# A one-core mixer block with split fp32 weights: order of the leading and trailing products, fewer LayerNorm visits, a shorter last normalisation

## The chip, the cores and the metric

One core of a Trainium2 chip runs the whole program. The metric is device time in microseconds (us) of one execution, less is better. Engines are called PE (TensorE matmul), PEld (its weight load), DVE (VectorE), ACT (ScalarE), POOL (GpSimd) and SP (SyncE), as the profile does.

## What is computed

One layer with 256 latent and 256 context tokens of 2048 channels. After RMSNorm and adaLN, one input projection feeds a convolution branch (GLU, depthwise convolution of width 31, LayerNorm over channels, swish, a SiLU gate) and a bidirectional gated recurrence; both go through a projection, are merged by sigmoid gates, and an output projection, a gated residual and a last RMSNorm follow:

```python
v = v + p["conv_dw_b"]
v = jax.nn.silu(layernorm(v, p["conv_ln_g"], p["conv_ln_b"]))
y_conv = (v * jax.nn.silu(z)) @ p["w_conv_out"]
y_rnn = ((hf + hb) * jax.nn.silu(z_r)) @ p["w_rnn_out"]
y = jax.nn.sigmoid(gc) * y_conv + jax.nn.sigmoid(gr) * y_rnn
x = x + gt[:, None] * (y @ p["w_o"])
return rmsnorm(x, final_g)
```

## The kernel before

Every fp32 weight and activation is split into a leading part (fp32r, "hi") and a remainder ("lo"), and a product is the sum of three: hi by hi, hi by lo, lo by hi. Weights come in slots `s` of 1 MB, each of two halves `h` (128 x 1024, 512 KB). `stage_load(s + 3)` has SP fetch the raw halves of a slot three ahead; `stage_split(s + 2, h)` splits a half two slots ahead: ACT copies it into `whi` (L184), and DVE subtracts that from the raw half into `wlo` (L189). To spare DVE, one half in four of the slots 24 to 103 (`adding`, L383) gets its `wlo` another way: ACT writes the negated, rounded weight into `wlo` (L195), and POOL then issues a DMA that adds the raw weight from HBM onto it (L196). There are four buffers of each kind, so the split of half (s + 2, h) starts when PE has read the half (s, h) for the last time.

The first 72 slots multiply weights as the stationary operand. The last 80 are five chunked stages of 16 slots, in the order gr, rnn, gc, conv, o: there the activations `xx` (`xh`, `xl`) are stationary, the weights stream with 512 columns, and the two token tiles `i` (128 tokens each) have one PSUM accumulator each. `chunk_mms` (L607) makes the six matmuls of one half for one token tile, and `chunk_slot` (L616) calls it for tile 0 and then tile 1:

```python
for w, y in ((hi, xh), (hi, xl), (lo, xh)):
    for kk in range(2): ...
```

so that a half is hi x4, lo x2 (tile 0), hi x4, lo x2 (tile 1). A chunk of 512 output columns takes four slots; then `evac` empties the two accumulators (DVE and ACT). The o stage does the same in its own loop (L1045 to L1067), and does its last two slots for tile 0 first, then tile 1.

The order of work on every engine is the order of the program. Between halves, `run_deferred` runs what was put off by a half, and `run_side` takes elementwise work (convolution taps on DVE, LayerNorm steps) from a queue, as much as a budget per slot allows. LayerNorm needs sums over channels, which are on partitions: `stat_mm` (L236) is an fp32 matmul with a 128 x 32 block of ones at column position 32 x (m mod 4), 256 columns wide, and shows as two instructions in the trace. For the means it is called in pairs of channel tiles (`mean`, L719: seven visits at tap 10 of the pairs, one at the end), for the variances once for each of 16 squares (`var`, L793), which run_deferred gathers into visits. After each sum a matmul with `sel4` adds the four quarters (`ln_total`), DVE copies the total to SBUF, and for the variance `rsqrt` (L205: ACT square root, DVE reciprocal and one Newton step) follows. Then the normalised tiles are gated and split; this must be done before the conv stage (L974).

In the o stage, `evac_o` (L1015) adds the residual, takes the square sum by ACT into `ssq`, and multiplies by the final weight; `finish` (L1032) computes the row's reciprocal root with `rsqrt`, scales the four column pieces on DVE and ACT in turn and has SP write them. `turn` (L978) transposes the merged result for the o stage while conv runs.

Of the kernel before, what the change touches and what calls it, by code (L numbers as in the profile page):

```python
# [15 lines left out]
P = 128  # L16
# [68 lines left out]
def block_kernel(ctx, tc, xcat, xtok, fgrow, brow, par, wada, wgt, bgt, wearly, wall, wgate, out):  # L85
# [335 lines left out]
    def defer(n, f):  # L421

        queue[n].append(f)
# [180 lines left out]
            k = 8 * half + kk  # L604
            PE.matmul(out=acc[:, 0], lhsT=lo[:, 128 * kk:128 * kk + 128], rhs=xh[:, k, 1], start=False, stop=(k == KT - 1))  # L605

    def chunk_mms(acc, s, seg, kq, h, i):  # L607

        hi, lo = parts[s, h]
        for w, y in ((hi, xh), (hi, xl), (lo, xh)):  # L610
            for kk in range(2):
                k = 4 * kq + 2 * h + kk
                PE.matmul(out=acc, lhsT=y[:, k, seg, P * i:P * i + P], rhs=w[:, 512 * kk:512 * kk + 512],  # L613
                          start=(k == 0 and w is hi and y is xh), stop=(k == KT - 1 and w is lo))

    def chunk_slot(s, seg, accs, kq, budget):  # L616

        stage_load(s + 3)
        for h in range(2):
            for i in range(2):  # L620
                chunk_mms(accs[i], s, seg, kq, h, i)
            del parts[s, h]
            stage_split(s + 2, h)
            run_deferred()
            run_side(budget / 2)
# [63 lines left out]
    def open_ph2():  # L689
        nonlocal cv, zc, tp2, p2  # L690
        ph1.close()
        cp = ph2.enter_context(tc.tile_pool(name="conv", bufs=1))
        tp2 = ph2.enter_context(tc.tile_pool(name="ctmp", bufs=2))
        cv = cp.tile([P, KT, T], F32, name="cv")
        zc = cp.tile([P, KT, T], F32, name="zc")
        p2 = cp.tile([P, KT, T], F32, name="p2")
        for n in ("rstd", "mean", "var"):
            ln[n] = tp2.tile([P, T], F32, tag=n, name=n, bufs=1)

    cv = zc = tp2 = p2 = mps = None  # L700
# [3 lines left out]
    def conv_ops(ms):  # L704
        ops = []

        def first(m):
            A.activation(out=cv[:, m], in_=vb[:, m], func=AF.Identity,  # L708
                         scale=hdw[:, m * CW + 15:m * CW + 16], bias=pc("dwb", m))

        def tapop(m, j):
            d = j - 15
            n = GW - abs(d)
            o0, i0 = max(0, -d), max(0, d)
            o = cv[:, m].rearrange("p (r c) -> p r c", c=GW)[:, :, o0:o0 + n]
# [3 lines left out]
        def mean(m):  # L719
            nonlocal mps  # L720
            if m == 0:
                mps = psum("mps")[:, :T]
            stat_mm(mps, cv[:, m], m)
# [52 lines left out]
        V.tensor_copy(ln["rstd"], mps)  # L776
        defer(0, ln_mean2)

    def ln_total(dst):
        tot = psum("tot")[:, :T]  # L780
        PE.matmul(out=tot, lhsT=sel4, rhs=ln["rstd"], start=True, stop=True)
        V.tensor_copy(dst, tot)

    def ln_mean2():
        ln_total(ln["mean"])
        side.extend((0.4, lambda m=m: ln_center(m)) for m in range(KT))

    def ln_center(m):
# [4 lines left out]
        def var():  # L793
            nonlocal vps
            if m == 0:
                vps = psum("vps")[:, :T]
            stat_mm(vps, sq, m)
            if m == KT - 1:
                defer(0, ln_var)
        defer(0, var)  # L800
# [203 lines left out]


    ssq = tp2.tile([P, 2, 4], F32, tag="ssq", name="ssq", bufs=1)
    rt = tp2.tile([P, 2], F32, tag="rt", name="rt", bufs=1)
    rn = tp2.tile([P, 2], F32, tag="rn", name="rn", bufs=1)
    ms2 = tp2.tile([P, 2, 2], F32, tag="ms2", name="ms2", bufs=1)
    A.activation(out=rn[:, 0:1], in_=epst, func=AF.Sqrt)  # L1010

    def ochunk(c, i):
        return xo[:, 2048 * i + 512 * c:2048 * i + 512 * c + 512]

    def evac_o(c, i, acc):  # L1015
        while c not in gt_done:
            gt_steps(1)
        o = ochunk(c, i)
        j = 2 * (2 * c + i)
        t = vb[:, j:j + 2].rearrange("p a t -> p (a t)")  # L1020
        V.scalar_tensor_tensor(out=t, in0=acc, scalar=0.5, in1=gtb[:, 512 * c:512 * c + 512], op0=MUL, op1=MUL)
        V.tensor_tensor(out=o, in0=o, in1=t, op=ADD)
        A.activation(out=t, in_=o, func=AF.Square, scale=2048.0 ** -0.5, accum_out=ssq[:, i, c:c + 1])
        V.tensor_tensor(out=o if c < 3 else last(i), in0=o, in1=fgb[:, 512 * c:512 * c + 512], op=MUL)
# [4 lines left out]
    def last(i):  # L1029
        return piece(p2v, 0, i)  # L1030

    def finish(i):  # L1032

        r, v = rn[:, i:i + 1], ms2[:, i, 1:2]
        V.tensor_tensor(out=v, in0=ms2[:, i, 0:1], in1=ssq[:, i, 3:4], op=ADD)
        rsqrt(r, rt[:, i:i + 1], v)
        for c in (3, 0, 1, 2):
            o = ochunk(c, i) if c < 3 else last(i)
            if c % 2:
                V.tensor_scalar(out=o, in0=o, scalar1=r, scalar2=None, op0=MUL)  # L1040
            else:
                A.activation(out=o, in_=o, func=AF.Copy, scale=r)
            SP.dma_start(out=out[i, :, 512 * c:512 * c + 512], in_=o)

    for c in range(4):  # L1045
        accs = [psum(f"o{c}{i}") for i in range(2)]
        for kq in range(2 if c == 3 else 4):
            stage_load(s + 3)
            for h in range(2):
                for i in range(2):  # L1050
                    chunk_mms(accs[i], s, 1, kq, h, i)
                del parts[s, h]
                stage_split(s + 2, h)
                gt_steps(GTO)
                if turns:
                    turn(turns.popleft())
            s += 1
        if c < 3:
            for i in range(2):
                evac_o(c, i, accs[i])  # L1060

    stage_split(NS, 0)
    for i in range(2):
        for q in range(2):
            for h in range(2):
                chunk_mms(accs[i], s + q, 1, 2 + q, h, i)
        evac_o(3, i, accs[i])  # L1067
        finish(i)
    ph2.close()
# [77 lines left out]
```

## Time and profile before

| what | value |
|---|---|
| median of 3 runs (lowest, highest) | 1137.34 us (1136.67, 1138.25) |
| the profiled execution, its own time | 1136.45 us |
| its span, first to last instruction | 1134.7 us |
| busy PE, PEld, DVE, ACT | 1103.8, 879.8, 902.8, 656.4 us |
| granted TensorE clock, mean | 0.993 |
| DMA, mean over the span | 226 GB/s |

The span leaves out 1.75 us of the execution's own time. The ends of matmuls are modelled: a matmul of 512 columns is shown as 0.39 us long though they follow each other faster, so starts are compared here, and a gap printed in brackets is shorter than the delay of the start. Rows of the timeline merge instructions of one kind; "x4" is four of them.

### The profile page before, as it was taken

What the parts mean: (1) busy time and instruction counts of PE and PEld (TensorE: products, weight loads), DVE (VectorE), ACT (ScalarE), POOL (GpSimd) and SP (SyncE); (2) the same over time, 40 slices, a digit from 0 to 9 for tenths busy, and PEclk for the clock granted to TensorE, in tenths of its full rate; (3) what the DMA queues carried; (4) which work ended last, traced back from release to release, by engine and by line L of the source; (5) the groups of instructions that cost most, each with busy time, mean ns of one, the idle gap of its engine ahead of it and who ended that gap; (6) DMA issues with size and microseconds to landing.
All of it is one profiled execution on the core that took longest, in us unless ns stands there. A gap on an engine that the chain in (4) does not pass through costs nothing.

```text
span 1134.7 us, 15866 instructions
## 1 busy us (share of the span) xinstructions
PE 1103.8 (97%) x5788; PEld 879.8 (78%) x5788; DVE 902.8 (80%) x1544; ACT 656.4 (58%) x894; POOL 34.8 (3%) x44
## 2 busy tenths in 40 slices
PE   6999999999999999999999999999999999999996
PEld 3777777777787888788888877777777888788885
DVE  5555577888799788889989889889986987888885
ACT  4222269867788889776565645545445854445443
POOL 0000000000000000000000000000000000000000
PEclk9999999999999999999999999999999999999999
DMA  9998534433355777878888887887885579888872
GB/s 375 367 407 325 236 113 128 131 119 124 100 163 171 211 216 196 234 204 236 240 215 245 224 246 217 218 227 224 219 242 162 159 244 343 304 307 298 279 278 93
DMA packets 74528, 256.45 MB, mean 226 GB/s; under 512 B 8273, under 2 KB 12497, under 8 KB 74065
## 3 DMA queue, kind: packets, MB, share of 16 engines
q1 hardware_dynamic: 68690, 234.47, 60.8%
q0 software_dynamic: 5760, 20.97, 10.2%
q8 instruction: 45, 0.74, 0.3%
q14 instruction: 33, 0.27, 0.1%
HBM read 253.31 MB, written 2.10 MB: 225 GB/s over the span
## 4 chain that ended last, share of the span: by engine, by line
PE 83%; DMA 9%; DVE 3%; ACT 2%; issue 2%; SPq 0%; ACTq 0%; DVEq 0%; POOLq 0%
PE y L613 20%; PE acc L602 19%; PE acc L605 10%; DMA wlo<-in_wall_dram 8%; PE acc L245 8%; PE o L613 8%; PE xr L245 6%; PE gate L491 5%; PE ada L220 3%; PE part L245 2%; DVE wlo L189 1%; DVE cv L717 1%; DMA xhi<-in_xcat_dram 1%; ACT whi L184 1%; ACT wlo L195 1%
## 5 line engine op out<-in xcount | busy, mean ns | idle before, releaser
L184 ACT ACTIVATE whi<-raw 128x1024 fp32r<-128x1024 f32 x304 | 321.2, 1058 | 315.4 <-PE y L613 88.2
L189 DVE TENSOR_TENSOR wlo<-raw,whi 128x1024 fp32r<-128x1024 f32 x264 | 321.1, 1219 | 72.4 <-ACT whi L184 71.7
L613 PE MATMUL y<-whi,xx 128*128 128x512 f32 x1024 | 278.1, 393 | 0.0
L602 PE MATMUL acc<-xx,whi 128*128 128x512 f32 x1024 | 265.3, 401 | 0.0
L613 PEld LDWEIGHTS y<-whi,xx 128*128 128x128 f32 x1024 | 191.4, 189 | 43.3 <-issue 4.1
L602 PEld LDWEIGHTS acc<-xx,whi 128*128 128x128 f32 x1024 | 185.6, 189 | 44.4 <-issue 9.6
L717 DVE SCALAR_TENSOR_TENSOR cv<-hbuf,pt,cv 128x196 f32<-128x196 f32 (+14 forms) x480 | 184.3, 446 | 12.3 <-ACT cv L708 11.8
L613 PE MATMUL y<-wlo,xx 128*128 128x512 f32 x512 | 159.7, 393 | 9.0 <-DMA wlo<-in_wall_dram 8.4
L605 PEld LDWEIGHTS acc<-xx,wlo 128*128 128x128 f32 x1024 | 139.4, 190 | 11.9 <-DMA wlo<-in_wall_dram 2.1
L605 PE MATMUL acc<-xx,wlo 128*128 128x256 f32 x1024 | 143.2, 283 | 0.6 <-DMA wlo<-in_wall_dram 0.6
L613 PEld LDWEIGHTS y<-wlo,xx 128*128 128x128 f32 x512 | 95.6, 189 | 33.4 <-DMA wlo<-in_wall_dram 12.8
L480 DVE SCALAR_TENSOR_TENSOR xc<-xr,pt,xc 128x510 f32<-128x510 f32 (+2 forms) x96 | 70.8, 741 | 0.2
L613 PE MATMUL o<-whi,xx 128*128 128x512 f32 x256 | 69.8, 394 | 0.0
L245 PE MATMUL acc<-xx,whi 128*128 128x512 f32 x256 | 65.2, 407 | 0.0
L245 PE MATMUL xr<-xx,whi 128*128 128x512 f32 x192 | 63.5, 412 | 0.0
L491 PE MATMUL gate<-xc,gw 128*128 128x512 f32 x128 | 60.0, 592 | 0.0
L196 POOL DMA_DIRECT2D wlo<-in_wall_dram x40 | 34.6, 866 | 805.1 <-ACT wlo L195 433.1
L245 PEld LDWEIGHTS acc<-xx,whi 128*128 128x128 f32 x256 | 47.8, 188 | 14.2 <-issue 4.8
L613 PEld LDWEIGHTS o<-whi,xx 128*128 128x128 f32 x256 | 47.7, 188 | 10.5 <-issue 1.0
L888 DVE SCALAR_TENSOR_TENSOR zc<-gtraw,csil,zc 128x512 f32<-128x512 f32 x64 | 47.9, 748 | 4.3 <-DMA zc<-in_bgt_dram 3.6
L344 ACT ACTIVATE row<-ada 128x128 f32<-128x128 f32 (+1 forms) x22 | 7.2, 326 | 62.3 <-PE ada L220 62.3
L195 ACT ACTIVATE wlo<-raw 128x1024 fp32r<-128x1024 f32 x40 | 41.9, 1047 | 0.8 <-PE acc L605 0.8
(181 smaller groups left out, 1061.1 us busy)
## 6 DMA issues: line engine op xcount, KB each, us to landing
raw<-in_wall_dram SPq DMA_DIRECT2D x304, 512.0 KB, 4.5
adaraw<-in_wada_dram SPq DMA_DIRECT2D x64, 512.0 KB, 7.6
wlo<-in_wall_dram POOLq DMA_DIRECT2D x40, 512.0 KB, 7.9
gtraw<-in_wgt_dram SPq DMA_DIRECT2D x32, 512.0 KB, 4.3
raw<-in_wearly_dram SPq DMA_DIRECT2D x16, 512.0 KB, 8.7
gw<-in_wgate_dram SPq DMA_DIRECT2D x32, 128.0 KB, 3.9
hbuf<-in_xcat_dram SPq DMA_DIRECT2D x2, 1024.0 KB, 6.3
gbias<-in_brow_dram SPq DMA_DIRECT2D x8, 256.0 KB, 5.8
```

Of the source, the lines that this page charges most:

```text
L184: A.activation(out=hi, in_=raw, func=AF.Copy)
L189: V.tensor_tensor(out=lo, in0=raw, in1=hi.bitcast(F32), op=SUB)
L195: A.activation(out=lo, in_=raw, func=AF.Copy, scale=-1.0)
L196: nc.gpsimd.dma_start(out=lo, in_=src, accum_op=ADD)
L245: PE.matmul(out=acc, lhsT=w, rhs=x, start=(first and i == 0), stop=(last and i == n - 1))
L480: V.scalar_tensor_tensor(out=o, in0=i, scalar=w, in1=o, op0=MUL, op1=ADD)
L491: PE.matmul(out=acc, lhsT=u["gw"][:, c:c + 128], rhs=u["xc"], start=True, stop=True)
L602: PE.matmul(out=acc, lhsT=hi[:, 128 * kk:128 * kk + 128], rhs=xx[:, k, 1], start=(k == 0), stop=False)
L605: PE.matmul(out=acc[:, 0], lhsT=lo[:, 128 * kk:128 * kk + 128], rhs=xh[:, k, 1], start=False, stop=(k == KT - 1))
L613: PE.matmul(out=acc, lhsT=y[:, k, seg, P * i:P * i + P], rhs=w[:, 512 * kk:512 * kk + 512], start=(k == 0 and w is hi and y is xh), stop=( ...
L717: V.scalar_tensor_tensor(out=o, in0=i, scalar=hdw[:, m * CW + j:m * CW + j + 1], in1=o, op0=MUL, op1=ADD)
L888: V.scalar_tensor_tensor(out=gt_chunk(c), in0=gt_raw[0][:, 512 * (k % 2):512 * (k % 2) + 512], scalar=csil[:, k, 0:1], in1=gt_chunk(c), op ...
```

## The change

1. `chunk_mms` gets an argument `leading`: either the four hi products of a token tile or its two lo products. A new `chunk_half` runs them in the order hi tile 0, hi tile 1, lo tile 0, lo tile 1. It serves all five chunked stages; only the last two slots of o keep the old order.
2. The sums for the mean run four tiles at a visit (four visits), those of the squares too (four visits; seven instead of six buffers for squares). The total of the variance is read from PSUM by `rsqrt` and not copied.
3. The last RMSNorm: the sum of the first three square sums, with EPS, is built up chunk by chunk; in `finish`, ACT's square root adds it as its bias, and DVE needs a reciprocal and two instructions after it, instead of one before the root and five after it. Pieces 0 and 2 (those that ACT scales) are written by DMAs that ACT issues, pieces 3 and 1 by SP.

```diff
-    def chunk_mms(acc, s, seg, kq, h, i):
-        hi, lo = parts[s, h]
-        for w, y in ((hi, xh), (hi, xl), (lo, xh)):
+    def chunk_mms(acc, s, seg, kq, h, i, leading):
+        w = parts[s, h][0 if leading else 1]
+        for y in (xh, xl) if leading else (xh,):
             for kk in range(2):
                 k = 4 * kq + 2 * h + kk
                 PE.matmul(out=acc, lhsT=y[:, k, seg, P * i:P * i + P], rhs=w[:, 512 * kk:512 * kk + 512],
...
+    def chunk_half(accs, s, seg, kq, h):
+        for leading in (True, False):
+            for i in range(2):
+                chunk_mms(accs[i], s, seg, kq, h, i, leading)
...
-            for i in range(2):
-                chunk_mms(accs[i], s, seg, kq, h, i)
+            chunk_half(accs, s, seg, kq, h)
...
-            if j == 10 and ms[0]:
-                for m in ms:
-                    ops.append((0.0, lambda m=m: mean(m - 2)))
+            if j == 10 and ms[0] and ms[0] % 4 == 0:
+                ops.append((0.0, lambda: means(ms[0] - 4)))
...
-            ops.append((0.0, lambda: defer(0, lambda: [mean(m) for m in ms])))
+            ops.append((0.0, lambda: defer(0, lambda: means(KT - 4))))
...
     def ln_center(m):
         V.tensor_tensor(out=cv[:, m], in0=cv[:, m], in1=ln["mean"], op=SUB)
-        sq = tp2.tile([P, T], F32, tag="sq", name="sq", bufs=6)
+        if m % 4 == 3:
+            variances()
+        sq = tp2.tile([P, T], F32, tag="sq", name="sq", bufs=7)
         A.activation(out=sq, in_=cv[:, m], func=AF.Square)
...
+        squares.append(sq)
+        if m % 4 == 3:
+            waiting.append((m - 3, squares[:]))
+            squares.clear()
+            defer(0, variances)
...
     def ln_rstd():
-        ln_total(ln["var"])
-        rsqrt(ln["rstd"], ln["mean"], ln["var"])
+        rsqrt(ln["rstd"], ln["mean"], ln_total())
...
-        if c == 2:
-            V.tensor_tensor(out=ms2[:, i, 0:1], in0=ssq[:, i, 0:1], in1=ssq[:, i, 1:2], op=ADD)
-            V.tensor_tensor(out=ms2[:, i, 0:1], in0=ms2[:, i, 0:1], in1=ssq[:, i, 2:3], op=ADD)
+        if c == 0:
+            V.tensor_scalar(out=ms2[:, i:i + 1], in0=ssq[:, i, 0:1], scalar1=EPS, scalar2=None, op0=ADD)
+        elif c < 3:
+            V.tensor_tensor(out=ms2[:, i:i + 1], in0=ms2[:, i:i + 1], in1=ssq[:, i, c:c + 1], op=ADD)
...
     def finish(i):
-        r, v = rn[:, i:i + 1], ms2[:, i, 1:2]
-        V.tensor_tensor(out=v, in0=ms2[:, i, 0:1], in1=ssq[:, i, 3:4], op=ADD)
-        rsqrt(r, rt[:, i:i + 1], v)
+        part, end = ms2[:, i:i + 1], ssq[:, i, 3:4]
+        v, r0, t, r = (rn[:, i, j:j + 1] for j in range(4))
+        A.activation(out=r0, in_=end, func=AF.Sqrt, bias=part)
+        V.tensor_scalar(out=v, in0=end, scalar1=part, scalar2=-0.5, op0=ADD, op1=MUL)
+        V.reciprocal(out=r0, in_=r0)
+        V.tensor_scalar(out=t, in0=v, scalar1=r0, scalar2=r0, op0=MUL, op1=MUL)
+        V.tensor_scalar(out=r, in0=t, scalar1=1.5, scalar2=r0, op0=ADD, op1=MUL)
...
-            SP.dma_start(out=out[i, :, 512 * c:512 * c + 512], in_=o)
+            (SP if c % 2 else A).dma_start(out=out[i, :, 512 * c:512 * c + 512], in_=o)
```

## Rows read from the trace of the kernel before

**Rows 1.** Busy time by stretch: us, busy (instructions) of each engine, PEclk, DMA share, GB/s.

```profile
474.00:658.00 184.00, 183.42 (x1041) 158.31 (x1041) 163.00 (x326) 115.23 (x158) 13.80 (x16) 1.00 0.83 229
658.00:860.00 202.00, 193.58 (x844) 153.22 (x843) 173.10 (x350) 98.48 (x110) 13.80 (x16) 0.99 0.80 223
860.00:1035.00 175.00, 173.76 (x782) 139.78 (x781) 139.65 (x199) 90.24 (x126) 0.00 (x0) 1.00 0.76 263
```

**Rows 2.** Waits of PE over the span: us in total, times, longest us.

```profile
PE y L613 <- DMA wlo<-in_wall_dram: 8.4, 10, 1.9
...
PE tps L982 <- DVE p L999: 0.7, 1, 0.7
...
PE y L613 <- DVE wlo L189: 0.6, 1, 0.6
```

**Rows 3.** Timeline of PE, gr stage: start us, us, what, idle before and releaser.

```profile
689.56 1.07 PE L613 MATMUL y<-whi,xx 128*128 128x512 f32 x4
692.18 0.73 PE L613 MATMUL y<-wlo,xx 128*128 128x512 f32 x2 [1.55 <-DMA wlo<-in_wall_dram]
692.76 1.08 PE L613 MATMUL y<-whi,xx 128*128 128x512 f32 x4
693.67 0.61 PE L613 MATMUL y<-wlo,xx 128*128 128x512 f32 x2
694.22 0.63 PE L239 MATMUL mps<-cv,ones 128*32 128x256 f32 x4
694.77 1.20 PE L613 MATMUL y<-whi,xx 128*128 128x512 f32 x4
695.81 0.62 PE L613 MATMUL y<-wlo,xx 128*128 128x512 f32 x2
```

**Rows 4.** The same timeline: four more of the ten waits for the DMA.

```profile
668.48 0.73 PE L613 MATMUL y<-wlo,xx 128*128 128x512 f32 x2 [0.91 <-DMA wlo<-in_wall_dram]
...
717.32 0.73 PE L613 MATMUL y<-wlo,xx 128*128 128x512 f32 x2 [1.81 <-DMA wlo<-in_wall_dram]
...
740.49 0.73 PE L613 MATMUL y<-wlo,xx 128*128 128x512 f32 x2 [0.30 <-DMA wlo<-in_wall_dram]
...
753.60 0.73 PE L613 MATMUL y<-wlo,xx 128*128 128x512 f32 x2 [1.92 <-DMA wlo<-in_wall_dram]
```

**Rows 5.** Timeline of ACT before the longest wait.

```profile
742.23 1.06 ACT L184 ACTIVATE whi<-raw 128x1024 fp32r<-128x1024 f32 x1 [2.26 <-PE y L613]
743.20 1.04 ACT L195 ACTIVATE wlo<-raw 128x1024 fp32r<-128x1024 f32 x1
```

**Rows 6.** Chain that ended last, same place: start us, us, what.

```profile
744.53 9.02 DMA wlo<-in_wall_dram
```

**Rows 7.** Busy time by stretch (columns as in rows 1) just after the longest wait.

```profile
754.60:758.00 3.40, 3.40 (x9) 2.64 (x8) 1.92 (x5) 2.26 (x3) 0.00 (x0) 0.51 0.28 107
```

**Rows 8.** Timeline of PE, gc stage: a visit with four variance sums.

```profile
861.79 0.64 PE L239 MATMUL vps<-sq,ones 128*32 128x256 f32 x8
862.36 1.20 PE L613 MATMUL y<-whi,xx 128*128 128x512 f32 x4
```

**Rows 9.** Chain that ended last, after the last matmul: start us, us, what.

```profile
1127.43 0.17 DVE ms L1035
...
1127.62 0.30 ACT rn L207
...
1128.15 0.17 DVE rt L209
```

**Rows 10.** Busy time by stretch (columns as in rows 1) while the last outputs are written.

```profile
1130.00:1133.20 3.20, 0.00 (x0) 0.00 (x0) 0.00 (x0) 0.26 (x1) 0.00 (x0) 0.52 0.87 328
```

**Rows 11.** Waits of ACT and of DVE from 655 to 860 us: us in total, times, longest us.

```profile
ACT whi L184 <- PE y L613: 76.1, 44, 4.3
...
DVE wlo L189 <- ACT whi L184: 14.5, 16, 2.2
```

**Rows 12.** Chain that ended last: 24 matmuls of 512 columns into one accumulator.

```profile
154.52 5.44 PE acc L245 x24
```

More of the change, by code (lines that the diff above doesn't have):

```diff
@@ L613, in chunk_mms @@
                 PE.matmul(out=acc, lhsT=y[:, k, seg, P * i:P * i + P], rhs=w[:, 512 * kk:512 * kk + 512],
-                          start=(k == 0 and w is hi and y is xh), stop=(k == KT - 1 and w is lo))
+                          start=(leading and k == 0 and y is xh), stop=(k == KT - 1 and not leading))
+    def chunk_half(accs, s, seg, kq, h):
+        for leading in (True, False):
+            for i in range(2):
+                chunk_mms(accs[i], s, seg, kq, h, i, leading)
     def chunk_slot(s, seg, accs, kq, budget):
@@ L696, in open_ph2 @@
         p2 = cp.tile([P, KT, T], F32, name="p2")
-        for n in ("rstd", "mean", "var"):
+        for n in ("rstd", "mean"):
             ln[n] = tp2.tile([P, T], F32, tag=n, name=n, bufs=1)
@@ L717, in tapop, with means @@
             V.scalar_tensor_tensor(out=o, in0=i, scalar=hdw[:, m * CW + j:m * CW + j + 1], in1=o, op0=MUL, op1=ADD)
-        def mean(m):
+        def means(k):
             nonlocal mps
-            if m == 0:
+            if k == 0:
                 mps = psum("mps")[:, :T]
-            stat_mm(mps, cv[:, m], m)
+            for m in range(k, k + 4):
+                stat_mm(mps, cv[:, m], m)
         for m in ms:
@@ L777, in ln_mean, with ln_total, variances @@
         defer(0, ln_mean2)
-    def ln_total(dst):
+    def ln_total():
         tot = psum("tot")[:, :T]
         PE.matmul(out=tot, lhsT=sel4, rhs=ln["rstd"], start=True, stop=True)
-        V.tensor_copy(dst, tot)
+        return tot
     def ln_mean2():
-        ln_total(ln["mean"])
+        V.tensor_copy(ln["mean"], ln_total())
         side.extend((0.4, lambda m=m: ln_center(m)) for m in range(KT))
+    squares, waiting = [], []
     def ln_center(m):
         V.tensor_tensor(out=cv[:, m], in0=cv[:, m], in1=ln["mean"], op=SUB)
-        sq = tp2.tile([P, T], F32, tag="sq", name="sq", bufs=6)
+        if m % 4 == 3:
+            variances()
+        sq = tp2.tile([P, T], F32, tag="sq", name="sq", bufs=7)
         A.activation(out=sq, in_=cv[:, m], func=AF.Square)
-        def var():
-            nonlocal vps
-            if m == 0:
+        squares.append(sq)
[3 more added lines that the diff above has]
+            defer(0, variances)
+    def variances():
+        nonlocal vps
+        while waiting:
+            k, sqs = waiting.pop()
+            if k == 0:
                 vps = psum("vps")[:, :T]
-            stat_mm(vps, sq, m)
-            if m == KT - 1:
+            for m, sq in enumerate(sqs, k):
+                stat_mm(vps, sq, m)
+            if k == KT - 4:
                 defer(0, ln_var)
-        defer(0, var)
     def ln_var():
@@ L1006, in block_kernel, with last @@
     ssq = tp2.tile([P, 2, 4], F32, tag="ssq", name="ssq", bufs=1)
[L1007 to L1010, printed above, removed]
+    rn = tp2.tile([P, 2, 4], F32, tag="rn", name="rn", bufs=1)
+    ms2 = tp2.tile([P, 2], F32, tag="ms2", name="ms2", bufs=1)
+    A.activation(out=rn[:, 0, 0:1], in_=epst, func=AF.Sqrt)
     def ochunk(c, i):
         return xo[:, 2048 * i + 512 * c:2048 * i + 512 * c + 512]
+    def last(i):
+        return piece(p2v, 0, i)
     def evac_o(c, i, acc):
@@ L1017, in evac_o @@
             gt_steps(1)
-        o = ochunk(c, i)
+        o, a, b = ochunk(c, i), 512 * c, 512 * c + 512
         j = 2 * (2 * c + i)
         t = vb[:, j:j + 2].rearrange("p a t -> p (a t)")
-        V.scalar_tensor_tensor(out=t, in0=acc, scalar=0.5, in1=gtb[:, 512 * c:512 * c + 512], op0=MUL, op1=MUL)
+        V.scalar_tensor_tensor(out=t, in0=acc, scalar=0.5, in1=gtb[:, a:b], op0=MUL, op1=MUL)
         V.tensor_tensor(out=o, in0=o, in1=t, op=ADD)
         A.activation(out=t, in_=o, func=AF.Square, scale=2048.0 ** -0.5, accum_out=ssq[:, i, c:c + 1])
-        V.tensor_tensor(out=o if c < 3 else last(i), in0=o, in1=fgb[:, 512 * c:512 * c + 512], op=MUL)
-        if c == 2:
-            V.tensor_tensor(out=ms2[:, i, 0:1], in0=ssq[:, i, 0:1], in1=ssq[:, i, 1:2], op=ADD)
-            V.tensor_tensor(out=ms2[:, i, 0:1], in0=ms2[:, i, 0:1], in1=ssq[:, i, 2:3], op=ADD)
-    def last(i):
-        return piece(p2v, 0, i)
-    def finish(i):
-        r, v = rn[:, i:i + 1], ms2[:, i, 1:2]
-        V.tensor_tensor(out=v, in0=ms2[:, i, 0:1], in1=ssq[:, i, 3:4], op=ADD)
-        rsqrt(r, rt[:, i:i + 1], v)
+        V.tensor_tensor(out=o if c < 3 else last(i), in0=o, in1=fgb[:, a:b], op=MUL)
+        if c == 0:
+            V.tensor_scalar(out=ms2[:, i:i + 1], in0=ssq[:, i, 0:1], scalar1=EPS, scalar2=None, op0=ADD)
+        elif c < 3:
+            V.tensor_tensor(out=ms2[:, i:i + 1], in0=ms2[:, i:i + 1], in1=ssq[:, i, c:c + 1], op=ADD)
+    def finish(i):
+        part, end = ms2[:, i:i + 1], ssq[:, i, 3:4]
[5 more added lines that the diff above has]
+        V.tensor_scalar(out=r, in0=t, scalar1=1.5, scalar2=r0, op0=ADD, op1=MUL)
         for c in (3, 0, 1, 2):
@@ L1049, in block_kernel @@
             for h in range(2):
-                for i in range(2):
-                    chunk_mms(accs[i], s, 1, kq, h, i)
+                chunk_half(accs, s, 1, kq, h)
                 del parts[s, h]
@@ L1065, in block_kernel @@
             for h in range(2):
-                chunk_mms(accs[i], s + q, 1, 2 + q, h, i)
+                for leading in (True, False):
+                    chunk_mms(accs[i], s + q, 1, 2 + q, h, i, leading)
         evac_o(3, i, accs[i])
```

## The prediction

> **What bounds the kernel now.** I read the busy time by stretch first. In the slots before the chunked stages (474 to 658 us) and from 860 us on PE is idle for about 1 us per stage; in gr and rnn (658 to 860 us) it is idle for 8.4 of 202 us [rows 1]. So PE sets the time nearly everywhere after the start, and what a change is worth is what it takes from PE's own sequence, plus the waits in gr and rnn, plus what comes after the last matmul. The waits of PE name the release: ten times it waited for the adding DMA of `wlo`, 8.4 us in all; once each for the transposed result and for DVE's `wlo` [rows 2].
>
> The timeline shows what one wait costs. Four hi matmuls take 0.91 us from start to start of the next run (692.76 to 693.67), 0.2275 us each, so two lo take 0.455. Behind the hi run at 689.56 the lo should start at 690.47; it starts at 692.18, 1.71 us late, where the printed gap is 1.55; and its two matmuls take 0.58 instead of 0.455 [rows 3]. A wait therefore costs its gap plus 0.16 plus 0.12. Ten of them: 8.4 + 10 x 0.28 = **11.2 us**.
>
> Why does that DMA come late? ACT's split of the next such half waited for PE and began at 742.23, its second copy at 743.20 [rows 5], POOL's DMA went out at 744.53 and took 9.02 us [rows 6]; PE needed it at about 751.5 and had it at 753.60 [rows 4]. ACT waited for PE 44 times, 76.1 us, in this stretch [rows 11]: the DMA is triggered by PE's last use of the leading half four halves earlier, and the race is between the transfer's latency and PE's progress.
>
> **The change, part by part.** All terms stand against the profiled execution's 1136.45 us; the median of the three runs is 0.9 above it, which I add at the end.
>
> *Leading products first.* The first lo matmul of a half comes after eight hi matmuls instead of four: 4 x 0.2275 = 0.91 us later. And the last hi matmul is the eighth of twelve instead of the tenth, so PE frees the `whi` buffer 0.455 us sooner; ACT, which waits for just that, starts both copies and the DMA as much sooner (the `wlo` buffer is still freed by the twelfth matmul, but by then ACT is busy with the first copy). The race gains 0.91 + 0.455 = 1.36 us per half. Lateness now is gap plus 0.16. The longest: 1.71 becomes 0.35 [rows 3], 1.97 becomes 0.61, 2.08 becomes 0.72 [rows 4]. The first (1.07) was triggered from the stationary-weight slots, whose order does not change: only 0.91 is gained, 0.16 is left. The wait at 740.49 (0.46) loses the cover of a LayerNorm visit that goes away (0.78, below): 0.46 + 0.78 - 1.36, still nothing; another of the short ones may share that. The five not shown sum to 8.4 - 6.5 = 1.9 and vanish. Left: 1.84 us plus four times 0.12, 2.3. Gain 11.2 - 2.3 = **8.9**. The same bytes must now move in some 6% less time with the DMA engines at 0.80 [rows 1]; if latencies grow by that share (0.4 to 0.5 us of 8 to 9), the waits that remain and one or two more cost 1.0: **7.9**. Bounds: 6.6 minus 1.0 = 5.6 if only the 0.91 counts; 11.2 if every wait goes. I take the middle, because both parts of the 1.36 follow from the program's order.
>
> *The clock after the longest wait.* Right after the wait of 1.92 us the granted clock was 0.51, the lower of the two levels (1.2 instead of 2.4 GHz), over 3.4 us, and PE began 9 matmuls where 3.4 / 0.2275 = 15 fit [rows 7]: 6 to 7 matmuls, 1.5 us. The wait of 1.81 was not followed by this. With no wait above 0.8 us left I count **1.5** gained; bounds 0 and 1.6.
>
> *Fewer visits for the sums.* A visit with two means: from the lo run at 693.67 to the next hi at 694.77 1.10 us instead of 0.455, and the next run 1.04 instead of 0.91: 0.78 us [rows 3]. A visit with four variance sums does not cost more: from its start to the next hi 0.57 us against 0.55 [rows 8]. So the price is per visit and not per tile. Means go from eight visits to four, squares from five (4, 4, 4, 3 and 1 tiles, as the budget of 1.5 per half cuts them) to four: 5 x 0.78 = **3.9**. All of them lie where PE is the bound [rows 1]. If merging four means costs a little (0.02 to 0.1 each) it is 3.5. The last mean visit and the last variance visit stay at their places in the program, so LayerNorm starts no later; the copy of the variance total that goes is DVE's and nobody on PE waits for it.
>
> *DVE's wait in gc.* The one late DVE `wlo` (gap 0.6, cost 0.88) is covered by the extra 0.91 us. But PE then reaches the first transpose sooner, where it waited 0.7 us for DVE [rows 2], and I count some of it back: **0.6**, bounds 0 and 1.7 (both waits gone).
>
> *The end.* After the last square sum the path is: DVE's add at 1127.43, root at 1127.62, reciprocal, then four small DVE steps of 0.17 + 0.02 [rows 9]. The add goes (0.19), as ACT's root takes the stored sum as bias; of the four steps two go (0.39). The product with -0.5 runs on DVE beside the root. **0.58** gained. The second queue I count at nothing: while the last outputs go out the DMA engines are 0.87 busy at 328 GB/s for the whole 3.2 us [rows 10], so the transfers follow each other without a hole, and the first cannot start before its piece is scaled. ACT's issue sits between its two scalings, but the third and fourth piece wait for the engines anyway. Bounds for the end: 0 (a queue's first use eats it) and 0.9. A rule of the Trainium skill bears on the queues: its page "DMA: Bandwidth & Descriptors", section "Issuing engines are not separate DMA queues", says that issuing from two engines saves only the sequencer's issue time. By it the end would gain one or two of SP's issue times, which lies inside the bound of 0.9; by the trace even this is hidden.
>
> *What else moves.* Tile 0's last matmul is now the tenth of a half and not the sixth, so its evacuation starts 0.9 us later and the pair ends up to 0.24 us later (DVE's first step of 0.69 no longer lies wholly before tile 1's end). Twenty chunks would make 4.8 us if nothing covered it; I take nothing, since PE waited for a DVE `wlo` only once [rows 2] and DVE itself waits for ACT [rows 11]. The new small adds in o follow a step that already waits for the same square.
>
> Sum: 7.9 + 1.5 + 3.9 + 0.6 + 0.6 = 14.5 us; 1136.45 - 14.5 = 1121.95, and on the scale of the median 1137.34 - 14.5 = **1122.8 us**.
>
> **Rivals.**
> *DVE becomes the bound in gr and rnn.* It is busy for 173.1 of 202 us [rows 1]; PE would now need about 202 - 7.9 - 1.5 - 1.6 = 191. For: 91% is much for an engine in program order. Against: its idle time is waiting for ACT's `whi`, which waits for PE [rows 11], and shrinks with it. If it took back all gains of that stretch, three visits, the gc wait and the end stay: 2.3 + 0.6 + 0.6 = 3.5, giving 1133.8 us. Chance 0.06.
>
> *Nothing is gained*: the DMA's landing moves with PE, every wait is back 1.36 us later, and the visits turn into longer waits. Then only the end is left, 1136.8 us. Against: the waits vary from 0.30 to 1.92 [rows 4] at one fixed place in the program, so a shift of the need is a real gain for the short ones. Chance 0.03.
>
> *Slower: changing the accumulator costs.* The new order changes between the two PSUM accumulators four times a half instead of twice, some 156 halves, 312 more changes. At 14.5 / 312 = 46 ns each the gains are gone; at 60 ns the time is 1122.8 + 18.7 = 1141.5 us. Against: 24 matmuls into one accumulator take 5.44 us, 0.227 each [rows 12], and the runs of four here, each of which begins with such a change, 0.2275 [rows 3]; a change now costs less than 5 ns. For: the Trainium skill, page "TensorE: Matmul & The Clock Gate", section "A second HAM failure mode: psum-queue depth-cycling", tells of a kernel with 512 columns whose walk through PSUM banks left small pauses between groups and made its clock fall again and again. By that rule this change would be slower; this trace, with 0.51 granted only after a wait, does not bear it out. Chance 0.03.
>
> **How the numbers follow.** The forecast has 0.88. The range: 5.6 + 0 + 3.5 + 0 + 0 = 9.1 us at the low end (1128.2), 11.2 + 1.6 + 3.9 + 1.7 + 0.9 = 19.3 at the high end (1118.0); not all bounds meet, so 1118.5 to 1128.5. About 0.2%, 2.3 us, is what a measurement of this kernel can tell from no change. Faster: the forecast, the DVE rival and a remainder, 0.94; the same 0.03; slower 0.03.
>
> **What would show it.** Right: waits of PE for the DMA of `wlo` down to 1 to 4 us in at most six places, none over 1 us; no stretch at the lower clock between 40 us and the end of the matmuls; eight visits with eight instructions each; halves in gr and rnn of 2.73 us; about 0.6 us less from the last square sum to the first scaling, and outputs that take as long from there as now. Wrong: PE waiting for DVE's `wlo` in rnn, runs of hi matmuls above 0.2275 us each, or new waits of PE in conv.

## The result, and the profile after

The changed kernel took 1124.73 us (median of 4 runs, 1123.41 to 1126.09) against 1137.01 us before (4 runs, 1136.48 to 1138.25): a ratio of 0.989, 95% interval 0.986 to 0.992, some 12.3 us less where 14.5 were forecast. Its profiled execution took 1123.41 us, with a span of 1121.6 us; set against the profiled execution of before that is 13.0 us less.

PE's waits over the span, the chunked stages' part of them (us in total, times, longest us), answering to [rows 2]:

```profile
PE y L613 <- DMA wlo<-in_wall_dram: 2.7, 4, 1.3
PE tps L998 <- DVE p L1015: 1.9, 3, 1.0
...
PE y L613 <- ACT whi L184: 0.8, 1, 0.8
...
PE y L613 <- DVE wlo L189: 0.3, 1, 0.3
```

The waits for the adding DMA fell from 8.4 us in ten to 2.7 us in four. The others, all in the second half of gc and in conv, grew from 1.3 to 3.0 us: in conv PE now waits 2.6 us in four places, where it waited 0.7 us in one before. Where the time went shows by stretch as in [rows 1], cut at this kernel's stages (us, busy and instructions of PE, PEld, DVE, ACT, POOL, PEclk, DMA share, GB/s):

```profile
655.00:840.00 185.00, 182.13 (x811) 147.36 (x811) 166.88 (x337) 93.71 (x100) 13.80 (x16) 1.00 0.86 240
840.00:1023.40 183.40, 180.35 (x813) 143.98 (x812) 144.22 (x208) 95.93 (x135) 0.00 (x0) 1.00 0.74 255
```

gr and rnn have PE idle for 2.9 us instead of 8.4 and no stretch at the lower clock; gc and conv have it idle for 3.1 us.

The timeline of PE at the place of [rows 3], two halves with a visit for the means between them:

```profile
684.64 1.98 PE L613 MATMUL y<-whi,xx 128*128 128x512 f32 x8
686.84 1.21 PE L613 MATMUL y<-wlo,xx 128*128 128x512 f32 x4 [0.22 <-DMA wlo<-in_wall_dram]
687.98 0.64 PE L239 MATMUL mps<-cv,ones 128*32 128x256 f32 x8
688.55 2.11 PE L613 MATMUL y<-whi,xx 128*128 128x512 f32 x8
690.50 1.08 PE L613 MATMUL y<-wlo,xx 128*128 128x512 f32 x4
```

Eight hi, four lo, and a visit with eight instructions, from whose start to the next hi it takes 0.57 us, as for the smaller visits before [rows 3, 8]. This is the half whose wait was 1.55 us. ACT at the same place, as in [rows 5]:

```profile
686.71 1.06 ACT L184 ACTIVATE whi<-raw 128x1024 fp32r<-128x1024 f32 x1 [1.66 <-PE y L613]
688.09 1.06 ACT L195 ACTIVATE wlo<-raw 128x1024 fp32r<-128x1024 f32 x1 [0.32 <-PE y L613]
```

ACT starts as the eighth hi matmul ends, before the first lo. Its second copy then waits 0.32 us for the `wlo` buffer, since the lo run itself was late; after a half without a wait it does not.

For what follows I counted halves in PE's timelines and took the time from the first matmul of gr (slot 72) to slot 112 in the middle of gc, and from there to the first of o (slot 136). From slot 136 to slot 144 every kernel takes 45.69 us. Slot 72 itself starts between 653.66 and 660.12 us in these profiles, for two reasons. The start-up, which the change leaves alone, ends earlier or later from one profile to the next: the first matmul of L602, a product with stationary weights, starts at 167.45 to 170.61 us. And two of the five visits that the change takes away lie before slot 72 (three visits for the means there before, at 569.03, 612.21 and 652.07 us; one after, at 608.29).

| kernel (one profile each) | slots 72 to 112, us | slots 112 to 136, us |
|---|---|---|
| before | 239.64 | 136.96 |
| after | 228.59 | 140.02 |

So the 13.0 us between the two profiles are 2.5 from the start-up (170.03 to 167.53 us at that first matmul), which the change did not bring, 2.2 from there to slot 72 (the two visits are 1.6 of them), 11.05 in slots 72 to 112, a loss of 3.1 in slots 112 to 136, and 0.4 at the end.

### The profile page after: what moved, and what is told of

Same layout as the page of the kernel before. It is cut to its first block, busy times and chain, and to the rows that moved or that the text cites. A ratio compares the mean times of both kernels' runs of the same rounds, so it can differ in the third digit from the quotient of the medians.

```text
span 1121.6 us, 15861 instructions
## 1 busy us (share of the span) xinstructions
PE 1094.8 (98%) x5788; PEld 876.6 (78%) x5788; DVE 900.6 (80%) x1541; ACT 657.5 (59%) x894; POOL 34.9 (3%) x44
## 4 chain that ended last, share of the span: by engine, by line
PE 79%; DMA 10%; DVE 5%; ACT 2%; issue 2%; SPq 0%; ACTq 0%; DVEq 0%; POOLq 0%
PE acc L602 20%; PE y L613 16%; PE acc L605 10%; PE acc L245 8%; PE o L613 8%; PE xr L245 6%; DMA wlo<-in_wall_dram 5%; PE gate L491 5%; DMA raw<-in_wall_dram 4%; PE ada L220 2%; PE part L245 2%; DVE wlo L189 2%; DVE zc L904 1%; ACT whi L184 1%; PE ms L239 1%
## 5 line engine op out<-in xcount | busy, mean ns | idle before, releaser
L602 PE MATMUL acc<-xx,whi 128*128 128x512 f32 x1024 | 265.0, 401 | 0.0
L613 PE MATMUL y<-whi,xx 128*128 128x512 f32 x1024 | 256.0, 392 | 0.8 <-ACT whi L184 0.8
L602 PEld LDWEIGHTS acc<-xx,whi 128*128 128x128 f32 x1024 | 185.7, 189 | 43.6 <-issue 9.6
L613 PE MATMUL y<-wlo,xx 128*128 128x512 f32 x512 | 137.9, 391 | 3.3 <-DMA wlo<-in_wall_dram 2.7
L613 PE MATMUL o<-whi,xx 128*128 128x512 f32 x256 | 65.3, 395 | 0.0
```

The source lines that it names most:

```text
L602: PE.matmul(out=acc, lhsT=hi[:, 128 * kk:128 * kk + 128], rhs=xx[:, k, 1], start=(k == 0), stop=False)
```

## The experiments

Each kernel's median stands against the kernel before in the same set of runs: 1136.33 us in the first (23 runs), 1135.71 in the second (20), 1137.27 in the third (17). Single executions of the kernel before spread from 1130.6 to 1142.4 us there, so differences of a microsecond or two are read from the profiles.

**Order alone.** The kernel before with `chunk_mms`, `chunk_half` and their calls as in the change, nothing else.

```diff
...
-            for i in range(2):
-                chunk_mms(accs[i], s, seg, kq, h, i)
+            chunk_half(accs, s, seg, kq, h)
```

> The kernel before with the new order of the products alone (leading parts of both token tiles first). Theory A (a race between the adding DMA and PE, and a loop of SP, DVE and DMA at the end of gc that takes part of the gain back): waits of PE for the DMA of wlo fall from 11 us of cost to 2 to 3, the low clock after the longest wait goes, and 1 to 3 us come back as waits for DVE or ACT between 900 and 970 us: 6 to 9 us faster than before. Theory C (the later end of tile 0's sums delays DVE): waits for DVE's wlo in gr and rnn, and less than 5 us gained. Without any give-back it would be 10 us.

Measured 1128.31 us, 8.0 less, ratio 0.992 (0.989 to 0.995). Slots 72 to 112 took 228.90 us, 112 to 136 took 138.20, 1.2 more than before. PE's waits from 655 to 850 us:

```profile
PE y L613 <- DMA wlo<-in_wall_dram: 1.7, 2, 1.1
```

That is all: nothing in gr or rnn waits for DVE, so theory C (tile 0's later end) is not borne out. The order is two thirds of the whole gain.

**LayerNorm alone.** The kernel before with the visits of four and the uncopied total:

```diff
-            if j == 10 and ms[0]:
+            if j == 10 and ms[0] and ms[0] % 4 == 0:
-                for m in ms:
-                    ops.append((0.0, lambda m=m: mean(m - 2)))
+                ops.append((0.0, lambda: means(ms[0] - 4)))
...
```

> The kernel before with the LayerNorm part alone (four visits each for means and squares, no copy of the variance total). Price per visit 0.78 us: five visits less are 3.9 us. But in the old order two of the removed visits gave the adding DMA 0.78 us of cover, before waits of 0.30 and 0.43 us: these waits should grow to about 1.1 and 1.2, so that 2.3 to 2.5 us are gained in all. If the price were per tile and not per visit, nothing would be gained by merging (0 us, or a loss of the 1.5).

Measured 1133.64 us, 2.7 less, ratio 0.998 (0.9955 to 1.000): the times hardly tell it from nothing. In its profile slots 72 to 112 took 236.03 us, 3.6 less, but a part of that is the lower clock of the profile before, which this one, with no wait above 1.5 us, does not show. Its waits for the DMA sum to 8.4 us as before, but they sit elsewhere; these are the two halves that lost a visit as cover (before: 0.30 and 0.43 us):

```profile
739.21 0.72 PE L613 MATMUL y<-wlo,xx 128*128 128x512 f32 x2 [1.24 <-DMA wlo<-in_wall_dram]
...
821.07 0.73 PE L613 MATMUL y<-wlo,xx 128*128 128x512 f32 x2 [1.11 <-DMA wlo<-in_wall_dram]
```

A visit is worth 0.78 us on PE, except where PE then only arrives earlier at a DMA that is on its way. With the new order these two halves wait 0.3 us at most in the three profiles of the changed kernel.

**End alone.** The kernel before with the new `evac_o` sums, `finish` and the two queues.

```diff
...
-        V.tensor_tensor(out=v, in0=ms2[:, i, 0:1], in1=ssq[:, i, 3:4], op=ADD)
-        rsqrt(r, rt[:, i:i + 1], v)
+        A.activation(out=r0, in_=end, func=AF.Sqrt, bias=part)
+        V.tensor_scalar(out=v, in0=end, scalar1=part, scalar2=-0.5, op0=ADD, op1=MUL)
+        V.reciprocal(out=r0, in_=r0)
+        V.tensor_scalar(out=t, in0=v, scalar1=r0, scalar2=r0, op0=MUL, op1=MUL)
+        V.tensor_scalar(out=r, in0=t, scalar1=1.5, scalar2=r0, op0=ADD, op1=MUL)
...
-            SP.dma_start(out=out[i, :, 512 * c:512 * c + 512], in_=o)
+            (SP if c % 2 else A).dma_start(out=out[i, :, 512 * c:512 * c + 512], in_=o)
```

> The kernel before with the last RMSNorm alone (shorter Newton step, ACT issues two of the four output DMAs). From the end of the last square sum to the first scaling 0.58 us less (now 1.51), outputs as long as before from there: 0.6 us faster, which the times cannot tell from nothing; the trace must show it. If the second queue helps, the last output lands another 0.3 us sooner; if ACT's issue hurts, later.

Measured 1135.66 us, 0.7 less, ratio 0.998 (0.996 to 1.0005): not told from nothing by the times. From the start of the last matmul to the end of the span it takes 9.48 us in this kernel and in the changed one, 9.88 in the kernel before: 0.40 us. The chain of the changed kernel after its last square sum, to be held against [rows 9]:

```profile
1114.79 0.30 ACT rn L1053
...
1115.12 0.18 DVE rn L1055
...
1115.32 0.28 DVE rn L1056
...
1115.63 0.23 DVE rn L1057
...
1115.88 0.73 ACT cv L1063
```

The add before the root is gone (0.19) and so are two of the four steps, but the two that remain, which read two and one per-partition scalars from SBUF, take 0.28 and 0.23 us instead of 0.17. From the root's start to the first scaling it is 1.09 us; before, from the add at 1127.43 to the first scaling at 1128.92, 1.49. The writing, over its own 2.9 us (same columns as in [rows 10]):

```profile
1117.20:1120.10 2.90, 0.00 (x0) 0.00 (x0) 0.00 (x0) 0.54 (x1) 0.00 (x0) 0.50 0.97 362
```

The DMA engines are no less full than before. From the first scaling to the end of the span it takes 5.7 to 5.8 us in both kernels (1115.88 to 1121.6; before, 1128.92 to 1134.7): the second queue gives nothing that can be seen.

This kernel's profile also shows the lower clock twice in gr and rnn, after waits of 1.91 and 1.84 us, and a third time in gc (0.50 from 934.7 to 937.9 us) after a wait of 1.97 us for DVE's `wlo`. The first wait's row, in PE's timeline, and the stretches behind the first two:

```profile
671.28 0.88 PE L613 MATMUL y<-wlo,xx 128*128 128x512 f32 x2 [1.91 <-DMA wlo<-in_wall_dram]
```

```profile
671.80:675.10 3.30, 3.30 (x9) 2.52 (x9) 2.26 (x7) 1.15 (x2) 0.00 (x0) 0.50 0.51 180
757.10:760.40 3.30, 3.30 (x10) 2.54 (x9) 1.54 (x4) 1.47 (x2) 0.00 (x0) 0.50 0.47 158
```

**Half the reordering.** In the changed kernel the half is run as hi tile 0, the two xh of tile 1, lo tile 0, the two xl of tile 1, lo tile 1:

```diff
-        for leading in (True, False):
-            for i in range(2):
-                chunk_mms(accs[i], s, seg, kq, h, i, leading)
+        for i, leading, ys in ((0, True, None), (1, True, (xh,)), (0, False, None), (1, True, (xl,)), (1, False, None)):
+            chunk_mms(accs[i], s, seg, kq, h, i, leading, ys)
```

> The changed kernel with half of the reordering: hi tile 0 (four), hi tile 1 (its two xh), lo tile 0, hi tile 1 (its two xl), lo tile 1. The first lo is the seventh matmul and the last hi the tenth: 0.455 us of the 1.36 us are kept. If the race is what matters, each lateness of the kernel before (1.07, 1.71, 0.35, 1.97, 0.46, 2.08, 0.40, 0.82, 0.59, 0.56, two of them 0.78 more for the visits that are gone) falls by 0.455 and 7 to 8 us of waits remain in gr and rnn: 4 to 7 us slower than the changed kernel, 1128 to 1132 us. If any separation of hi and lo is enough, it is as fast as the changed kernel (1124 to 1125).

Measured 1129.09 us, 6.6 less than before, ratio 0.994 (0.992 to 0.997): it gains some 4.6 to 5.7 us less than the changed kernel does in its own sets of runs, as the race says. Slots 72 to 112 took 234.99 us, between 228 and 240. The waits over the span:

```profile
PE y L613 <- DMA wlo<-in_wall_dram: 7.3, 10, 1.5
```

**Need earlier than trigger.** One hi matmul is put behind the four lo, so that the first lo is the eighth matmul, but `whi` is read until the twelfth:

```diff
+        order = [(0, 0, xh, 0), (0, 0, xh, 1), (0, 0, xl, 0), (0, 0, xl, 1), (1, 0, xh, 0), (1, 0, xh, 1), (1, 0, xl, 0),
+                 (0, 1, xh, 0), (0, 1, xh, 1), (1, 1, xh, 0), (1, 1, xh, 1), (1, 0, xl, 1)]
...
```

> The changed kernel with one hi matmul (tile 1's last xl) put behind the four lo: the first lo is the eighth matmul of a half (0.68 us later than in the kernel before), but the buffer of whi is freed by the twelfth (0.455 us later than before, 0.91 later than in the changed kernel). If the trigger counts as much as the need, only 0.23 us of the 1.36 are left and the waits are nearly those of the LayerNorm part alone: 7 to 9 us of gaps in 9 to 11 waits, 1129 to 1133 us. If only the place of the first lo counts, it lies between the half-way kernel (1129.1) and the changed one: 3 to 5 us of gaps, 1126 to 1127.5 us.

Measured 1132.44 us, 4.8 less than before, ratio 0.996 (0.993 to 0.998). Waits from 650 to 850 us:

```profile
PE y L622 <- DMA wlo<-in_wall_dram: 7.0, 9, 1.5
```

This kernel needs the lo parts 0.23 us earlier than the changed one and frees `whi` 0.91 us later, and its waits are nearly those of the old order. The earlier need alone could add at most 9 x 0.23 = 2.1 us to the gaps of the nine halves that wait; against the 2.0 to 3.5 us of the changed kernel's three profiles they are 3.5 to 5.0 us longer. So the earlier release of the buffer is a real part of the gain. Against the half-way kernel, whose first lo is the seventh matmul, it is not placed: their intervals overlap, its slots 72 to 112 took 234.10 us against 234.99, and its profile holds a wait of 2.09 us for DVE's `wlo` in gc with the lower clock behind it (0.50 from 922.1 to 925.4 us), outside the slots that the DMA adds to.

**A change of accumulator at every matmul.** The changed kernel with the tiles alternating inside the hi and the lo runs, twelve changes a half:

```diff
-        for leading in (True, False):
-            for i in range(2):
-                chunk_mms(accs[i], s, seg, kq, h, i, leading)
+        for w, y in zip((0, 0, 1), (xh, xl, xh)):
+            for kk in range(2):
+                k = 4 * kq + 2 * h + kk
+                for i in range(2):
+                    PE.matmul(out=accs[i], lhsT=y[:, k, seg, P * i:P * i + P], rhs=parts[s, h][w][:, 512 * kk:512 * kk + 512],
...
```

> The changed kernel with the accumulator changed at every matmul (tile 0, tile 1, tile 0, ...), still hi before lo: 12 changes a half instead of 4, about 1250 more. The price of a change that the rows of before allow is under 5 ns: at most 6 us more, and I expect nothing, 1124 to 1126 us, with halves of 2.72 us. If a change cost the 46 ns at which the slower rival decides, it would be 57 us more.

Measured 1123.22 us, ratio 0.990 (0.987 to 0.992). Its PE timeline:

```profile
701.47 1.98 PE L622 MATMUL y<-whi,xx 128*128 128x512 f32 x8
703.28 1.07 PE L622 MATMUL y<-wlo,xx 128*128 128x512 f32 x4
704.19 1.98 PE L622 MATMUL y<-whi,xx 128*128 128x512 f32 x8
```

A half of 2.72 us (701.47 to 704.19): a change costs nothing that can be measured, and the slower rival's price is out. Its other half, the clock, needs a look, since this profile has one stretch at the lower clock, in conv. The stretch, and PE's waits from 930 to 960 us:

```profile
956.50:959.70 3.20, 3.20 (x9) 2.46 (x9) 2.76 (x4) 2.39 (x3) 0.00 (x0) 0.50 0.89 319
```

```profile
PE tps L1001 <- DVE p L1018: 1.6, 2, 1.0
```

It begins just after these two waits for the transposed result (0.62 us before the matmul at 953.87, 0.99 before that at 955.19), and no other stretch between 40 us and the last matmul has the lower clock, though every half changes accumulator as often. The Trainium skill, "TensorE: Matmul & The Clock Gate", section "A second HAM failure mode: psum-queue depth-cycling", tells of a kernel of 512 columns whose walk through PSUM banks makes PE pause so often that its clock goes down and up. No run here shows that of two accumulators that take turns, with fp32r weights in a kernel as full as this one.

**The changed kernel again, twice.** The same kernel without any edit, once in the first set of runs and once in the third.

> The changed kernel once more, for a second profile of it. Theory A: the lead over the kernel before, about 15 us at the middle of gc, shrinks again by 2 to 4 us in the last slots of gc and the first of conv, by waits for whi, wlo and the transposed result. Theory B (chance in the landing times of that place): the shrinking differs by more than 2 us from the first profile's 3, or is not there.

> The changed kernel, third profile. Lead over the kernel before at the middle of gc 11 to 16 us (start-up differs by up to 4), and a shrinking of 0 to 3 us between slots 116 and 128; waits for the DMA of wlo in gr and rnn 1.5 to 3.5 us in 3 to 6 places, the first of them always at the first adding half of gr, whose trigger lies in the older order.

Measured 1124.64 us (ratio 0.989, 0.985 to 0.992) and 1126.09 us (0.990, 0.987 to 0.992). Slots 72 to 112 took 227.53 and 229.39 us, much as in the first profile; slots 112 to 136 took 137.33 and 139.96, so 0.4 and 3.0 us more than in the profile of before. The second profile is what theory B expected, the first and the third are what theory A says: the size of the loss changes from profile to profile. The third's lead at slot 112 was 10.7 us (897.96 to 887.23), just under the 11 to 16 expected. The waits for the DMA over the span, in the second profile and in the third:

```profile
PE y L613 <- DMA wlo<-in_wall_dram: 2.0, 4, 0.7
```

```profile
PE y L613 <- DMA wlo<-in_wall_dram: 3.5, 3, 2.1
```

The third had one wait of 2.05 us that the others do not have: the transfer, issued at 705.86 us, took 10.5 us to land, where that of the same half took 8.9 in the other two. The clock stayed at 1.00 behind it:

```profile
716.40 1.21 PE L613 MATMUL y<-wlo,xx 128*128 128x512 f32 x4 [2.05 <-DMA wlo<-in_wall_dram]
```

```profile
717.40:721.00 3.60, 3.60 (x17) 2.94 (x17) 0.00 (x0) 2.57 (x4) 0.86 (x1) 1.00 0.42 102
```

A wait of that size does not bring the lower clock every time.

**The gate weights on POOL's queue.** What holds slots 112 to 136 back? The chain that ended last in the changed kernel's first profile, from 912 to 960 us, by line and one of its pieces:

```profile
by line: DMA raw<-in_wall_dram 58.3%; DVE zc L904 14.0%; DVE wlo L189 9.9%; ACT whi L184 8.6%; issue 7.4%; SPq L892 2.0%; SPq L929 0.9%; ACTq L184 0.2%; DVEq L189 0.2%; SPq L179 0.1%; DVEq L904 0.0%
...
917.35 7.24 DMA raw<-in_wall_dram
```

PE is not in it. SP's own timeline says why:

```profile
913.26 0.35 SPq L892 DMA_DIRECT2D gtraw<-in_wgt_dram  x1
913.71 1.09 SPq L179 DMA_DIRECT2D raw<-in_wall_dram  x2
914.85 0.42 SPq L943 DMA_DIRECT2D gbias<-in_brow_dram  x1
916.97 0.33 SPq L892 DMA_DIRECT2D gtraw<-in_wgt_dram  x1
917.35 1.22 SPq L179 DMA_DIRECT2D raw<-in_wall_dram  x2
923.79 0.33 SPq L892 DMA_DIRECT2D gtraw<-in_wgt_dram  x1
924.21 1.04 SPq L179 DMA_DIRECT2D raw<-in_wall_dram  x2
```

Each pair of raw loads stands in the queue behind a load of the residual gate's weights (gtraw), which waits until DVE has used an earlier one; DVE in turn stands behind a `wlo` that waits for ACT, which waits for raw. The edit, made to both kernels, takes the two gate loads off SP:

```diff
-        SP.dma_start(out=raw, in_=wgt[n])
+        nc.gpsimd.dma_start(out=raw, in_=wgt[n])
...
-        SP.dma_start(out=gtb[0:1, :], in_=bgt)
+        nc.gpsimd.dma_start(out=gtb[0:1, :], in_=bgt)
```

> The changed kernel with the gate weights (gtraw, bgt) fetched by POOL's queue, so that SP's raw loads no longer stand behind a gtraw load that waits for DVE. Theory A (this loop takes back gains): no waits for DVE, ACT or the transposed result between slots 116 and 126, ACT's waits for raw there gone: 1 to 3 us faster than the changed kernel. Theory B: the waits there are chance and small, under 1 us on the median. A cost may come from POOL's slower issue (0.86 us each): then waits of DVE for gtraw.

> The kernel before with the same move of the gate weights to POOL's queue. Its two waits at that place (for DVE's wlo, 0.9 us of cost, and for the transposed result, 0.9) should go: 1 to 2 us faster than before, 1134 to 1135.5 us. If the move itself costs, both of these kernels are slower by the same.

> The changed kernel with the gate weights on POOL's queue, beside the changed kernel itself under one set of runs. Theory A: 2 to 4 us faster than the changed kernel, and in its profile a lead that grows by about 1 us between the middle of gc and the second conv chunk. Theory B: within 1 us of it, and its lead shrinks there as often as it grows.

Measured: changed kernel with the move 1120.99 us (ratio 0.9875, 0.985 to 0.990) and, beside the unmoved one at 1126.09, 1119.82 us (0.984, 0.982 to 0.987); old order with the move 1133.51 us (0.998, 0.996 to 1.000). The 6.3 us against the unmoved kernel in the same set are more than the 2 to 4 expected; against that kernel's third profile, slots 112 to 136 give 4.9 and slots 72 to 112 give 2.1, and in the latter the moved kernel's own two profiles differ by 2.8, so only the 4.9 can be put down to the move. In all three profiles slots 112 to 136 take 135.05 us. SP and POOL of the moved kernel's second profile at the same place, a fence each:

```profile
896.33 17.19 SPq L179 DMA_DIRECT2D raw<-in_wall_dram  x7
913.57 0.43 SPq L943 DMA_DIRECT2D gbias<-in_brow_dram  x1
914.33 13.57 SPq L179 DMA_DIRECT2D raw<-in_wall_dram  x7
```

```profile
912.32 0.55 POOL L892 DMA_DIRECT2D gtraw<-in_wgt_dram  x1 [5.32 <-DVE zc L904]
916.05 0.53 POOL L892 DMA_DIRECT2D gtraw<-in_wgt_dram  x1 [3.17 <-DVE zc L904]
```

and PE's busy time from 880 us to the o stage in its first profile, with no idle time at all:

```profile
880.00:1023.00 143.00, 143.00 (x638) 117.34 (x637) 120.91 (x166) 74.95 (x99) 11.10 (x21) 1.00 0.83 294
```

The wait for DVE is now POOL's, which has nothing else queued there. Theory A holds: the loop through SP's queue cost 1.9 us in the kernel before (136.96 - 135.05) and 5.0, 2.3 and 4.9 us in the three profiles of the changed one. Whether it costs more after the change is not settled. Five profiles of old or half-changed orders with the loads on SP give 1.9 to 4.0 us, five of the new order 2.3 to 5.0. In three of them (end alone, need earlier than trigger, accumulator at every matmul) a stretch at the lower clock lies in slots 112 to 136 and is part of the figure. The old order with the move is the one kernel that waits in the o stage (0.73 us for DVE's `wlo`), and its way from slot 136 to the last matmul is 90.90 us instead of 89.88. The profiles, in us:

| kernel | slots 72 to 112 | slots 112 to 136 |
|---|---|---|
| end alone | 241.37 | 138.95 |
| LayerNorm alone | 236.03 | 137.85 |
| half the reordering | 234.99 | 137.31 |
| need earlier than trigger | 234.10 | 139.03 |
| order alone | 228.90 | 138.20 |
| accumulator at every matmul | 227.65 | 138.73 |
| after, again and third | 227.53, 229.39 | 137.33, 139.96 |
| old order, gate weights on POOL | 238.40 | 135.05 |
| new order, gate weights on POOL, two profiles | 230.14, 227.33 | 135.05, 135.05 |

The changed kernel with the gate weights on POOL is the fastest of all here: 17 us less than before in one set of runs and 15 in the other, and beside the changed kernel its interval lies wholly below (0.9819 to 0.9867 against 0.9874 to 0.9922).

## Why the prediction held, point by point

**Leading products first: right, and for the reason given.** The forecast left 2.3 us of cost in four waits, 3.3 with an allowance for longer landings. The three profiles of the changed kernel have gaps of 2.7, 2.0 and 3.5 us in four, four and three places, so with 0.28 each 3.8, 3.1 and 4.3: the allowance was needed. The 0.91 us from the later need and the 0.455 from the earlier trigger were both counted as real, and the half-way and the late-trigger kernel bear that out. The sum came out better than its pieces. The first wait, forecast to leave 0.16 us because its trigger lies in the older order, is the one that never goes: its gap is 0.74, 0.66 and 0.75 us in the changed kernel. The longest wait of before, forecast to leave 0.72 us, is gone in all three. And the sign "none over 1 us" failed twice: 1.28 us in the first profile and 2.05 in the third, at halves whose transfers took 9.7 and 10.5 us to land where the same half's took 7.5 to 8.1 and 8.9 in the other two. The allowance for longer landings had the right size, but they come singly and not as a share on all.

**The clock: the result was right, its condition was not.** None of the changed kernel's three profiles shows the lower clock between 40 us and the last matmul. But the forecast rested on no wait above 0.8 us being left, and there were waits of 1.28 and 2.05 us, so in the third profile the 1.5 us came by luck. Nor does the size of one wait decide it: the lower clock followed waits of 1.92 us in the kernel before and of 1.84, 1.91, 1.97, 2.08 and 2.09 in three others, and two waits of 0.62 and 0.99 us in the kernel that changes accumulator at every matmul; it did not follow waits of 1.81 us (before) and 2.05 (changed, third).

**Visits: right.** Four visits instead of eight for the means and four instead of five for the squares, at one price. Two of the five that went lie before slot 72. From slot 72 to 112 the terms of the forecast (waits 7.9, clock 1.5, three of the five visits 2.3) make 11.7 us; measured 11.05, 12.1 and 10.25 us against the profile of before. The side effect named for the wait at 740 us showed when the visits went alone: 1.24 us.

**DVE's wait in gc: wrong.** The forecast counted 0.6 us gained, as the step "PE then reaches the first transpose sooner, and I count some of it back". In its place slots 112 to 136 took 0.4 to 3.1 us more than in the profile of before. I had treated the two waits there as two events, one covered by the new order and one to be reached sooner; they are the surface of one loop of SP, DVE, DMA and ACT that runs at its own pace, near PE's, for a dozen slots. Ahead of it, PE's gain of 0.9 us for the first lo is of use only until the loop's lag exceeds it. The bounds (0 and 1.7) left out a loss, although the trace of before, from 915 to 972 us, already showed ACT waiting for raw loads and SP's gate loads waiting for DVE:

```profile
ACT whi L184 <- DMA raw<-in_wall_dram: 21.0, 11, 7.4
```

```profile
SPq L876 <- DVE zc L888: 32.7, 9, 5.8
```

New waits of PE in conv were also one of the forecast's own signs of being wrong, and they came: 2.6 us there in the first profile against 0.7 before. That the loop through SP's queue is what costs is shown by the move of the gate weights; how PE's lead is lost to it, slot by slot, is my reading of the chain and not measured.

**The end: right in kind, 0.40 us instead of 0.58.** The term that was mis-sized is the two DVE steps, taken at 0.17 us; with scalars from SBUF they take 0.28 and 0.23. The queue was rightly counted at nothing.

**What was counted at nothing** stayed so: no wait for DVE in gr and rnn, none for evacuations. The parts alone add up to 8.0 + 2.7 + 0.7 = 11.4 us, the whole to 11.2 to 12.3, so the forecast of 14.5 is 2 to 3 us too high. By stretch most of that is the place after slot 112: forecast 0.6 us gained, measured 0.4 to 3.1 lost, 1.0 to 3.7 us apart. The rest, slots 72 to 112 among it, differs by 1.5 us or less in any one stretch and not always the same way. That the time came within the range is due to the large terms being right and this one being small beside them.

## What to carry to other kernels

When a consumer waits for a buffer that is refilled on its own release, moving the need later and the last use earlier add up: order the reads so that the buffer that triggers the refill is finished first. A wait that a profile shows once may be the visible tip of a queue that runs level with the bound engine; before counting it as covered, read the chain there, and look for a load that stands behind another load's wait in one queue. Small work that interrupts a dense run of matmuls costs per interruption, so gather it, but not where the interruption was the cover of a transfer.

## What the runs showed that I had not expected

- A DVE step on one column with scalars from SBUF takes 0.28 us with two of them and 0.23 with one (the other operation's being a constant), where 0.17 was seen for one with tensor operands or constants alone.
- The start-up, the same code in every kernel, ends up to 3.2 us earlier or later between profiles (first matmul of L602 at 167.45 to 170.61 us), so single profiles must be compared from a common point.
- Two waits of under 1 us, 0.62 and 0.99, with one transpose between them were followed by 3.2 us at a granted clock of 0.50, while a single wait of 2.05 us elsewhere was not.
- POOL's plain loads of 512 KB were no burden: the two gate loads on its queue left PE without any idle time from 880 to 1023 us in the changed kernel's order.
